# Differential attention on TensorE: both score products of a head ahead of their two masks, and the rotary products of q and k in one instruction each

## The chip, the cores and the metric

The program runs on one core of a Trainium2 chip. The metric is the device time of one execution in microseconds (us), as a median over runs. A profiled execution has a span of its own, from its first instruction to its last, and a time of its own that is a little longer than the span.

## The reference, cut to what matters

A trunk of two layers works on 272 rows (16 learned tokens and 256 inputs) of width 1024. Each layer has a mixer, a layer norm, a feed-forward part (dense in layer 0, eight experts with the two best chosen in layer 1) and a layer norm. The change lies in the attention half of the mixer: four heads, each with two query and key sets of width 64 and one set of values of width 128.

```python
def apply_rope(x, cos, sin):
    x1, x2 = jnp.split(x, 2, axis=-1)
    return x * c + jnp.concatenate([-x2, x1], axis=-1) * s
...
s = jnp.einsum('bqhcd,bkhcd->bhcqk', qb, k).astype(jnp.float32) * scale
causal = kpos[None, :] <= qpos[:, None]
p = jax.nn.softmax(jnp.where(causal, s, -jnp.inf), axis=-1)
a = p[:, :, 0] - lam * p[:, :, 1]
return jnp.einsum('bhqk,bkhe->bqhe', a.astype(v.dtype), v)
```

## The kernel before

**Blocks and slots.** Each mixer first computes its input projection as 24 column blocks in a fixed order (`IN_ORDER`, k and q of heads 0 and 1 first). A block is 24 matmuls on PE: eight slices of the inner dimension, each as three products (`hh`·`whi`, `hl`·`whi`, `hh`·`wlo`, lines 284, 285, 287). The weights arrive by DMA as `raw`; ACT rounds them to `whi` (line 145) and DVE forms the rest `wlo` (line 152), some blocks ahead of PE. The order of all else is written by hand: `Q.at(i, f)` runs step f behind block i, on whichever engines f uses, and the evictions of the blocks follow. Every engine then works through its own instructions in that order.

**The steps of a head b.** `qk[b]` is one tile of 128 partitions by 2 by 272: index 0 holds q, index 1 holds k; partitions 0 to 63 belong to the first of the two sets (c = 0), 64 to 127 to the second (c = 1). `swap` copies `qk[b]` to `rot[b]` by four DMAs with the halves of each 64 exchanged. `rope_cos` multiplies `qk[b]` by the cosines on POOL (line 547), in two instructions, k and then q. `rope` multiplies `rot[b]` by the sines and adds it to `qk[b]` on DVE (lines 553 and 555), in four instructions. In layer 1 the first 16 columns of q aren't needed: a memset has set them to zero, and the instructions on q start at column 16.

**Scores.** `scores(b)` runs behind blocks 10, 12, 14 and 16. It takes up to three tiles t of query rows: 128 rows against 272 keys, 128 rows against 144, and in layer 0 alone 16 rows against 16. For each t and each c it multiplies q by k over 64 partitions in f32 (line 609; each shows as two matmuls in the trace) into the PSUM bank of c, and then adds the causal mask to the diagonal part by a bf16 product of an identity with the mask (line 611). DVE takes the negated row maxima (`mx`, line 621), ACT the exponentials with their sums (line 623). `diff(b)`, one block later, subtracts the second map from the first on DVE (line 634); `a_T(b)`, two blocks behind `scores(b)`, transposes the result on PE (lines 643 to 648); `values(b)` follows a block later.

Of the kernel before, what the change touches and what calls it, by code (L numbers as in the profile page):

```python
# [16 lines left out]
ALU = mybir.AluOpType  # L17
# [3 lines left out]
P = 128  # L21
# [4 lines left out]
T = NMETA + SEQ  # L26
# [161 lines left out]
def body(tc, h0T, consts, vecs, lamv, w_in, w_out, w_gu, w_dn, w_r, mixgb, w_g, w_u, w_d, out, dbg=None):  # L188
    nc = tc.nc
    with ExitStack() as ctx:  # L190
# [9 lines left out]
        def nm(s):  # L200
            uid[0] += 1
            return f"{s}_{uid[0]}"
# [55 lines left out]
        cos = cpre[:, C_COS - C_PRE:C_COS - C_PRE + T]  # L258
        sin = cpre[:, C_SIN - C_PRE:C_SIN - C_PRE + T]
# [12 lines left out]
        def bank(tag="mm", bufs=3):  # L272
            return ps.tile([P, 512], F32, tag=tag, bufs=bufs, name=nm("ps"))
# [220 lines left out]
        def mixer(l, S, Q, before_out=None):  # L494
            c0 = 0 if l == 0 else NMETA
            nq = T - c0
            n2 = max(c0 - 2, 0)
            with tc.tile_pool(name=f"atz{l}", bufs=1) as zp:
# [23 lines left out]
                qk = {}  # L522
# [11 lines left out]
                rot = {}  # L534

                def swap(b):
                    rot[b] = ap.tile([P, 2, T], F32, tag="rot", bufs=2, name=nm("rot"))
                    for p0 in (0, 64):
                        for hf in range(2):
                            d0, s0 = p0 + 32 * hf, p0 + 32 * (1 - hf)  # L540
                            nc.sync.dma_start(rot[b][d0:d0 + 32], qk[b][s0:s0 + 32])

                def rope_cos(b):
                    for j in (1, 0):
                        n0 = c0 if j == 0 else 0
                        x = qk[b][:, j, n0:]
                        nc.gpsimd.tensor_tensor(x, x, cos[:, n0:], ALU.mult)

                def rope(b):
                    for j in (1, 0):  # L550
                        n0 = c0 if j == 0 else 0
                        r = rot[b][:, j, n0:]
                        nc.vector.tensor_tensor(r, r, sin[:, n0:], ALU.mult)
                        x = qk[b][:, j, n0:]
                        nc.vector.tensor_tensor(x, x, r, ALU.add)

                vts = {}

# [44 lines left out]
                def scores(b):  # L603
                    s = [bank("s", 2) for c in range(2)]
                    views = [[s[c][:, :272], s[c][:, 272:416], s[c][:, 416:432]] for c in range(2)]
                    for t, (q0, qn, kn) in enumerate(qt):
                        for c in range(2):
                            pr = slice(c * 64, (c + 1) * 64)
                            nc.tensor.matmul(views[c][t][:qn], qk[b][pr, 0, q0:q0 + qn], qk[b][pr, 1, :kn],
                                             start=True, stop=False)  # L610
                            nc.tensor.matmul(views[c][t][:qn, kn - qn:kn], identb[:qn, :qn], maskb[:qn, :qn],
                                             start=False, stop=True)
                    mx = ap.tile([P, 3, 2], F32, tag="mx", bufs=2, name=nm("mx"))
                    e1 = ap.tile([P, 2, 272], F32, tag="e1", bufs=1, name=nm("e1"))
                    e2 = ap.tile([P, 320], F32, tag="e2", bufs=1, name=nm("e2"))
                    ev = [e1, e2[:, 0:288].rearrange("p (c k) -> p c k", c=2),
                          e2[:, 288:320].rearrange("p (c k) -> p c k", c=2)]
                    es_[b] = ev
                    for t, (q0, qn, kn) in enumerate(qt):
                        for c in range(2):  # L620
                            nc.vector.tensor_reduce(mx[:qn, t, c:c + 1], views[c][t][:qn], AX.X, ALU.max, negate=True)
                        for c in range(2):
                            nc.scalar.activation(ev[t][:qn, c], views[c][t][:qn], AF.Exp, bias=mx[:qn, t, c:c + 1],
                                                 accum_out=sums[:qn, b, t, c:c + 1])
# [75 lines left out]
                for b in range(4):  # L700
                    i = (4, 5, 10, 12)[b]
                    Q.at(i, swap, b)
                    Q.at(i + 1, rope_cos, b)
                    Q.at((8, 9, 12, 14)[b], rope, b)
                    Q.at((8, 9, 14, 15)[b], v_T, b)
                    i = 10 + 2 * b
                    Q.at(i, scores, b)
                    Q.at(i + 1, diff, b)
                    Q.at(i + 2, a_T, b)
                    Q.at(i + 3, values, b)  # L710
                    Q.at(order.index(("h", b)) + 1, conv, b)
# [7 lines left out]
                for i, (t, b) in enumerate(order):  # L719
                    w = W.next()  # L720
                    n0 = c0 if t in "qb" else n2 if t in "ch" else 0
# [99 lines left out]
        Q.at(8, lambda_vals)  # L821
        ln_follow(S0, Q, AF.Exp, 1)
        S1 = mixer(0, S0, Q)
        lpx.close()

# [100 lines left out]
        def prefetch():  # L926
# [3 lines left out]
            W.pump()  # L930

        S3 = mixer(1, S2, Q, prefetch)
        lp = S3.lp
        pre.close()
# [476 lines left out]
```

## Time and profile before

| | us |
|---|---|
| median of 3 runs | 1513.78 |
| lowest and highest run | 1509.94, 1514.09 |
| the profiled execution's own time | 1512.59 |
| its span | 1510.7 |

PE is the TensorE matmul row and PEld its weight loads; matmul durations overlap in the records, so the distance between two starts tells more than the length of one. DVE is VectorE, ACT ScalarE, POOL GpSimd. PE counts as busy for 97% of the span, DVE for 81%, ACT for 66%, POOL for 7%. The input projection and attention of layer 0 lie in the first 130 us, those of layer 1 between some 366 and 467 us, and the experts fill the span from about 500 us on.

### The profile page before, as it was taken

What the parts mean: (1) busy time and instruction counts of PE and PEld (TensorE: products, weight loads), DVE (VectorE), ACT (ScalarE), POOL (GpSimd) and SP (SyncE); (2) the same over time, 40 slices, a digit from 0 to 9 for tenths busy, and PEclk for the clock granted to TensorE, in tenths of its full rate; (3) what the DMA queues carried; (4) which work ended last, traced back from release to release, by engine and by line L of the source; (5) the groups of instructions that cost most, each with busy time, mean ns of one, the idle gap of its engine ahead of it and who ended that gap; (6) DMA issues with size and microseconds to landing.
All of it is one profiled execution on the core that took longest, in us unless ns stands there. A gap on an engine that the chain in (4) does not pass through costs nothing. (4 is left out here: it accounts for less than half of the span.)

```text
span 1510.7 us, 20551 instructions
## 1 busy us (share of the span) xinstructions
PE 1472.8 (97%) x8085; PEld 1272.6 (84%) x8085; DVE 1220.3 (81%) x1210; ACT 998.9 (66%) x1089; POOL 99.1 (7%) x109
## 2 busy tenths in 40 slices
PE   9999999999999899999999999999999999999996
PEld 8789899999889787888888888888888888888885
DVE  7867875465876688898898888889879889888885
ACT  6665464344565577777777777776777777777773
POOL 1202200022102410000000000000000000000001
PEclk9999999999999899999999999999999999999998
DMA  7433264353437588999999999999999999998970
GB/s 258 151 122 138 99 257 151 116 167 155 162 140 277 182 328 334 370 344 376 365 367 364 380 344 348 372 369 359 380 344 347 376 369 370 372 361 333 362 290 30
DMA packets 65240, 427.96 MB, mean 283 GB/s; under 512 B 7520, under 2 KB 11616, under 8 KB 15344
## 3 DMA queue, kind: packets, MB, share of 16 engines
q1 hardware_dynamic: 64672, 426.20, 75.6%
q8 instruction: 65, 1.06, 0.3%
q10 hardware_dynamic: 432, 0.35, 0.1%
q14 instruction: 39, 0.32, 0.1%
q0 software_dynamic: 32, 0.03, 0.0%
HBM read 423.27 MB, written 1.05 MB: 281 GB/s over the span
## 5 line engine op out<-in xcount | busy, mean ns | idle before, releaser
L174 DVE TENSOR_TENSOR wlo<-raw,whi 128x2048 fp32r<-128x2048 f32 x332 | 755.1, 2296 | 119.2 <-ACT whi L173 119.1
L173 ACT ACTIVATE whi<-raw 128x2048 fp32r<-128x2048 f32 x332 | 632.0, 1922 | 152.7 <-PE ps L1069 152.0
L1067 PE MATMUL ps<-whi,xg 128*128 128x512 f32 x896 | 355.6, 397 | 0.0
L1069 PE MATMUL ps<-whi,xg 128*128 128x512 f32 x896 | 350.7, 391 | 2.9 <-POOL xg L1044 2.9
L1068 PE MATMUL ps<-wlo,xg 128*128 128x512 f32 x896 | 350.3, 391 | 0.0
L284 PE MATMUL ps<-hh,whi 128*128 128x272 f32 (+4 forms) x736 | 219.4, 298 | 3.4 <-ACT whi L145 1.5
L285 PE MATMUL ps<-hl,whi 128*128 128x272 f32 (+4 forms) x736 | 216.6, 295 | 4.0 <-DVE hl L394 3.7
L287 PE MATMUL ps<-hh,wlo 128*128 128x272 f32 (+4 forms) x720 | 210.8, 293 | 1.8 <-DVE wlo L152 1.8
L1069 PEld LDWEIGHTS ps<-whi,xg 128*128 128x128 f32 x896 | 168.8, 188 | 39.8 <-POOL xg L1044 3.8
L1067 PEld LDWEIGHTS ps<-whi,xg 128*128 128x128 f32 x896 | 169.2, 189 | 33.1
L152 DVE TENSOR_TENSOR wlo<-raw,whi 128x1024 fp32r<-128x1024 f32 (+2 forms) x148 | 170.3, 1173 | 33.0 <-ACT whi L145 32.9
L1068 PEld LDWEIGHTS ps<-wlo,xg 128*128 128x128 f32 x896 | 169.2, 189 | 32.9
L1069 PE MATMUL ps<-whi,aTl 128*128 128x512 f32 x448 | 174.9, 390 | 2.3 <-DVE aTl L277 2.2
L1067 PE MATMUL ps<-whi,aTh 128*128 128x512 f32 x448 | 175.6, 392 | 0.5 <-ACT aTh L276 0.5
L1068 PE MATMUL ps<-wlo,aTh 128*128 128x512 f32 x448 | 174.7, 390 | 0.0
L145 ACT ACTIVATE whi<-raw 128x1024 fp32r<-128x1024 f32 (+2 forms) x148 | 144.5, 990 | 45.4 <-PE ps L285 37.6
L285 PEld LDWEIGHTS ps<-hl,whi 128*128 128x128 f32 x736 | 142.6, 194 | 6.7 <-DVE hl L394 5.4
L284 PEld LDWEIGHTS ps<-hh,whi 128*128 128x128 f32 x736 | 142.6, 194 | 5.3 <-ACT whi L145 1.7
L287 PEld LDWEIGHTS ps<-hh,wlo 128*128 128x128 f32 x720 | 139.4, 194 | 2.4 <-DVE wlo L152 2.4
L1069 PEld LDWEIGHTS ps<-whi,aTl 128*128 128x128 f32 x448 | 84.1, 188 | 21.1 <-DVE aTl L277 3.6
L1067 PEld LDWEIGHTS ps<-whi,aTh 128*128 128x128 f32 x448 | 84.2, 188 | 17.5 <-ACT aTh L276 0.7
L1068 PEld LDWEIGHTS ps<-wlo,aTh 128*128 128x128 f32 x448 | 84.3, 188 | 16.7
(260 smaller groups left out, 1478.2 us busy)
## 6 DMA issues: line engine op xcount, KB each, us to landing
raw<-in_w_g_dram SPq DMA_DIRECT2D x112, 1024.0 KB, 7.1
raw<-in_w_u_dram SPq DMA_DIRECT2D x112, 1024.0 KB, 7.0
raw<-in_w_d_dram SPq DMA_DIRECT2D x112, 1024.0 KB, 7.2
raw<-in_w_in_dram SPq DMA_DIRECT2D x23, 1024.0 KB, 5.1
raw<-in_w_gu_dram SPq DMA_DIRECT2D x22, 1024.0 KB, 4.8
raw<-in_w_dn_dram SPq DMA_DIRECT2D x16, 704.0 KB, 4.1
raw<-in_w_out_dram SPq DMA_DIRECT2D x8, 1024.0 KB, 4.8
rot<-qk SPq DMA_DIRECT2D x32, 68.0 KB, 4.5
```

The costliest lines, as they stand in the source:

```text
L145: self.nc.scalar.activation(hi, raw, AF.Copy)
L152: self.nc.vector.tensor_tensor(lo, raw, hi.bitcast(F32), ALU.subtract)
L173: self.nc.scalar.activation(hi, raw, AF.Copy)
L174: self.nc.vector.tensor_tensor(lo, raw, hi.bitcast(F32), ALU.subtract)
L284: nc.tensor.matmul(o, w.hi[:, k], xh(k0 + k), start=first and i == 0, stop=False)
L285: nc.tensor.matmul(o, w.hi[:, k], xl(k0 + k), start=False, stop=False)
L287: nc.tensor.matmul(o, w.lo[:, k], xh(k0 + k), start=False, stop=last and i == ka - 1)
L1067: nc.tensor.matmul(o, xh, whi, start=first, stop=False)
L1068: nc.tensor.matmul(o, xh, wlo, start=False, stop=False)
L1069: nc.tensor.matmul(o, xl, whi, start=False, stop=last)
```

## The change

The loop over the two sets c is cut in two, so that for each t both score products are issued first and both masks behind them. The rotary products lose their loop over q and k: one instruction covers both, with the table of cosines or sines repeated by an operand of step 0. In layer 1 these instructions now also cover the first 16 columns of q.

```diff
+                def both(t):
+                    return t.rearrange("p (j t) -> p j t", j=1).to_broadcast([P, 2, T])
+
                 def rope_cos(b):
-                    for j in (1, 0):
-                        n0 = c0 if j == 0 else 0
-                        x = qk[b][:, j, n0:]
-                        nc.gpsimd.tensor_tensor(x, x, cos[:, n0:], ALU.mult)
+                    nc.gpsimd.tensor_tensor(qk[b], qk[b], both(cos), ALU.mult)
 
                 def rope(b):
-                    for j in (1, 0):
-                        n0 = c0 if j == 0 else 0
-                        r = rot[b][:, j, n0:]
-                        nc.vector.tensor_tensor(r, r, sin[:, n0:], ALU.mult)
-                        x = qk[b][:, j, n0:]
-                        nc.vector.tensor_tensor(x, x, r, ALU.add)
+                    nc.vector.tensor_tensor(rot[b], rot[b], both(sin), ALU.mult)
+                    nc.vector.tensor_tensor(qk[b], qk[b], rot[b], ALU.add)
...
                             nc.tensor.matmul(views[c][t][:qn], qk[b][pr, 0, q0:q0 + qn], qk[b][pr, 1, :kn],
                                              start=True, stop=False)
+                        for c in range(2):
                             nc.tensor.matmul(views[c][t][:qn, kn - qn:kn], identb[:qn, :qn], maskb[:qn, :qn],
                                              start=False, stop=True)
```

On PE the place is `scores(0)` of layer 0. Before, the tile of 144 keys stood as follows (`qk_287` is head 0, `ps_691` and `ps_692` are the banks of c = 0 and c = 1; a score product is one row here):

```order
L609 MATMUL ps_691<-qk_287 128x144
L611 LDWEIGHTS identb
L611 MATMUL ps_691<-maskb,identb 128x128
L609 MATMUL ps_692<-qk_287 128x144
L611 LDWEIGHTS identb
L611 MATMUL ps_692<-maskb,identb 128x128
```

Now the same tile reads (the banks have become `ps_685` and `ps_686`, and line 611 has become 608):

```order
L605 MATMUL ps_685<-qk_287 128x144
L605 MATMUL ps_686<-qk_287 128x144
L608 LDWEIGHTS identb
L608 MATMUL ps_685<-maskb,identb 128x128
L608 LDWEIGHTS identb
L608 MATMUL ps_686<-maskb,identb 128x128
```

The product of c = 1 has moved ahead of the mask of c = 0; number and sizes are the same, and so it goes in every tile of every head.

On DVE the place is the rotary part of heads 0 and 1 in layer 0, ahead of the row maxima of head 0. Before (`cpre` holds the sines, `qk_345` and `rot_460` belong to head 1):

```order
L553 TENSOR_TENSOR rot_414<-rot_414,cpre 128x272
L555 TENSOR_TENSOR qk_287<-qk_287,rot_414 128x272
L553 TENSOR_TENSOR rot_414<-rot_414,cpre 128x272
L555 TENSOR_TENSOR qk_287<-qk_287,rot_414 128x272
L152 TENSOR_TENSOR wlo_613<-raw_348,whi_612 128x8x128
L553 TENSOR_TENSOR rot_460<-rot_460,cpre 128x272
L555 TENSOR_TENSOR qk_345<-qk_345,rot_460 128x272
L553 TENSOR_TENSOR rot_460<-rot_460,cpre 128x272
L555 TENSOR_TENSOR qk_345<-qk_345,rot_460 128x272
```

Now:

```order
L550 TENSOR_TENSOR rot_414<-rot_414,cpre 128x544
L551 TENSOR_TENSOR qk_287<-qk_287,rot_414 128x544
L152 TENSOR_TENSOR wlo_609<-raw_348,whi_608 128x8x128
L550 TENSOR_TENSOR rot_459<-rot_459,cpre 128x544
L551 TENSOR_TENSOR qk_345<-qk_345,rot_459 128x544
```

Four instructions of 272 columns have become two of 544 in each head, and nothing has changed its place among the others.

## Rows read from the trace of the kernel before

**Rows 1.** The page, part 1: busy time, share of the span, instructions.

```profile
PE 1472.8 (97%) x8085; PEld 1272.6 (84%) x8085; DVE 1220.3 (81%) x1210; ACT 998.9 (66%) x1089; POOL 99.1 (7%) x109
```

**Rows 2.** PE's waits, 50 to 115 us, then 400 to 460 us.

```profile
PE ps L566 <- ACT aT L654: 0.9, 1, 0.9
...
PE ps L287 <- DVE wlo L152: 0.7, 1, 0.7
```

**Rows 3.** Timeline of PE: scores(0) of layer 0 (start, length, engine, line).

```profile
56.07 0.29 PE L285 MATMUL ps<-hl,whi 128*128 128x272 f32 x1
56.20 0.29 PE L287 MATMUL ps<-hh,wlo 128*128 128x272 f32 x1
56.42 0.72 PE L609 MATMUL ps<-qk 64*128 64x272 f32 x2
57.08 0.23 PE L611 MATMUL ps<-maskb,identb 128*128 128x128 bf16 x1
57.24 0.72 PE L609 MATMUL ps<-qk 64*128 64x272 f32 x2
...
58.05 0.51 PE L609 MATMUL ps<-qk 64*128 64x144 f32 x2
58.49 0.23 PE L611 MATMUL ps<-maskb,identb 128*128 128x128 bf16 x1
58.65 0.51 PE L609 MATMUL ps<-qk 64*128 64x144 f32 x2
...
59.25 0.21 PE L609 MATMUL ps<-qk 64*16 64x16 f32 x2
59.40 0.17 PE L611 MATMUL ps<-maskb,identb 16*16 16x16 bf16 x1
59.49 0.21 PE L609 MATMUL ps<-qk 64*16 64x16 f32 x2
...
59.74 0.39 PE L284 MATMUL ps<-hh,whi 128*128 128x272 f32 x1
```

**Rows 4.** Timeline of PE: the end of scores(0) of layer 1.

```profile
406.31 0.51 PE L609 MATMUL ps<-qk 64*128 64x144 f32 x2
406.75 0.23 PE L611 MATMUL ps<-maskb,identb 128*128 128x128 bf16 x1
406.79 0.37 PE L284 MATMUL ps<-hh,whi 128*128 128x256 f32 x1
```

**Rows 5.** Timeline of DVE: first sine product, next `wlo`, differences of head 0.

```profile
52.52 0.44 DVE L553 TENSOR_TENSOR rot<-rot,cpre 128x272 f32<-128x272 f32 x1
...
54.33 1.22 DVE L152 TENSOR_TENSOR wlo<-raw,whi 128x1024 fp32r<-128x1024 f32 x1
...
65.33 0.91 DVE L634 SCALAR_TENSOR_TENSOR e<-e,cf 128x272 f32<-128x272 f32 x3
```

**Rows 6.** Timeline of PE: first transpose of head 0.

```profile
65.96 0.41 PE L643 MATMUL ps<-cst,e 128*128 128x128 f32 x2
```

**Rows 7.** DVE's waits, 50 to 115 us.

```profile
DVE mx L621 <- PE ps L611: 5.2, 3, 2.2
```

**Rows 8.** Timelines of POOL (cosines of head 2) and DVE (their first use).

```profile
66.33 2.38 POOL L547 TENSOR_TENSOR qk<-qk,cpre 128x272 f32<-128x272 f32 x2 [20.00 <-DMA rot<-qk]
...
73.51 0.44 DVE L555 TENSOR_TENSOR qk<-qk,rot 128x272 f32<-128x272 f32 x1
```

**Rows 9.** Windows: length, busy time of five engines, PE's granted clock, DMA share, GB/s.

```profile
59.70:63.10 3.40, 3.40 (x28) 3.38 (x28) 1.63 (x6) 3.02 (x13) 0.00 (x0) 1.00 0.88 308
...
80.70:84.10 3.40, 3.40 (x21) 1.98 (x19) 1.19 (x4) 0.53 (x2) 0.10 (x1) 1.00 0.47 157
84.10:88.60 4.50, 4.50 (x25) 4.50 (x24) 3.44 (x11) 3.70 (x14) 0.00 (x0) 0.62 0.27 115
...
404.10:407.00 2.90, 2.90 (x15) 1.70 (x15) 1.43 (x2) 0.30 (x2) 0.00 (x0) 1.00 0.75 209
```

## The prediction

> **What bounds the kernel now.** I read the busy times of the whole span first, then PE's waits in the two stretches that the change touches, and then PE's timeline there, start by start. PE is busy for 97% of the span [rows 1]. Where the scores lie it hardly ever waits: one wait of 0.9 us between 50 and 115 us, and a longest one of 0.7 us between 400 and 460 us; the first is for a copy of transposed scores, the second for a weight split ahead of the first score product [rows 2]. So PE's own order is the bound there, and a shorter stretch on PE moves all that follows it, up to the end of the program.
>
> The timeline shows what a score product costs beyond its columns. Blocks of 128 rows follow each other at 0.13 us, but from the last of them (56.20) to the first score product, which uses 64 rows, it takes 0.22 us: 0.09 us more [rows 3]. From there to the mask it takes 0.66 us with 272 columns and 0.44 us with 144 [rows 3]. The difference of 0.22 us is two matmuls of 128 columns, so one pass is 0.23 us for 272 columns and 0.12 us for 144, and a fixed 0.19 us is left in both (0.66 - 0.47, 0.44 - 0.25). I split it into the 0.09 us seen at the change of rows and 0.10 us for a first weight load with nothing ahead of it to hide behind. The tile of 16 columns has 0.15 us, of which some 0.12 is fixed. From a mask to the next score product it takes 0.16 us, or 0.09 with 16 columns [rows 3]. Where a mask is followed by a matmul of the same 128 rows, that matmul's record starts 0.04 us after it [rows 4]. So PE pays at each change between 64 and 128 rows, and before, each of the two sets pays twice.
>
> **The change on PE.** Per tile there were four such changes and two are left: into the pair of score products, and out of it. The second score product of a pair then costs its two passes alone, which saves the fixed 0.19 us. The first mask is followed by the second, of the same rows, so 0.09 of its 0.16 us goes. That is 0.28 us for each of the two large tiles and 0.12 + 0.09 = 0.21 for the small one. A head of layer 0 saves 0.77 us, one of layer 1 (no small tile) 0.56; four of each make 5.3 us.
>
> No row of this trace has two products in a row on different halves of the 64-row arrangement, so this term has bounds. The least: a change of half costs as much as a change of rows, and its load is not hidden. Then only the 0.09 us behind the first mask is saved, 8 x 2 + 4 = 20 times, or 1.8 us. The most: the passes of the second set also run while those of the first do. Then one pass more per pair goes, at most 0.23 + 0.12 us per head, 2.8 us in all, and the term is 8.1. I take 5.3: what costs time in the rows is the change between 64 and 128 rows, and loads between matmuls of one arrangement are hidden in every block [rows 3].
>
> The rows show that a change of rows is paid; they don't show whether a change of half is. The Trainium skill, "TensorEngine Tiling (Array Packing)", section Key Properties, says that changing the tiling mode drains TensorE, and that going to another tile of the same mode does not. By it the term is 5.3 us; by the most cautious reading of the rows alone it is 1.8. No run shows this yet.
>
> **What follows on DVE.** The first row maximum of a head waits for the last mask in the bank of c = 0, which the change brings closer to the end of the group; the group ends earlier by 0.56 to 0.77 us, so that mask is still earlier than before. DVE idles for it in three of the four heads of layer 0, 5.2 us in all [rows 7], so its chain of maxima, exponentials and differences moves forward with PE. Behind these maxima on DVE stand weight splits, and PE doesn't run short of these behind the first score product [rows 2].
>
> Head 0 of layer 0 is the one place where DVE isn't waiting. Its first difference starts at 65.33 and is done some 0.44 us later (three together take 0.91), and PE's first transpose starts at 65.96, 0.19 us behind [rows 5, 6]. PE would come 0.77 us earlier and find nothing. Here the rotary part pays: one head takes 1.81 us on DVE (52.52 to 54.33) [rows 5]. A product of 272 columns is 0.44 us and one of 1024 is 1.22, so a column costs 1.0 ns and 544 columns 0.72 us. With the hop of about 0.1 us between the two and the overlap of 0.08 us at the end, two instructions make 1.46: 0.35 us less per head. Two heads stand ahead of the maxima of head 0, so the chain comes 0.7 us earlier, and PE loses 0.1 us. In the other seven heads the saving on DVE is worth nothing on the path, as PE or ACT sets their pace; without it head 0 would give back 0.7 us.
>
> **POOL.** Two products of 272 columns take 2.38 us with the gap between them; the result is first used at 73.51, 4.8 us after they end at 68.71 [rows 8]. One of 544 columns has the same elements. I put it between half the time (all of it a fixed cost per instruction) and twice the time (the repeated operand read badly), and take the time of now. At twice it would end at 71.1, still 2.4 us early. It costs nothing on the path. The 16 more columns of q in layer 1 are 0.02 us on DVE per instruction.
>
> **The clock.** Behind two of the four groups of scores of layer 0 PE's granted clock is at the lower level, 1.2 GHz, for a while: behind the group of head 2 (80.7 to 84.1, at 1.00) the stretch of 4.5 us has a mean of 0.62 [rows 9]; head 3's, at 98.4 us, reads the same. There 25 matmuls take 4.5 us; at the rate at full clock (28 in 3.4 us) [rows 9] they would take 3.0. Each such stretch costs 1.5 us. Behind the four groups of layer 1, which last 2.7 to 2.9 us and not 3.3 to 3.4, the clock stays at 1.00 (the group of head 0 stands in [rows 9]). After the change a group of layer 0 lasts 3.3 - 0.77 = 2.5 us, shorter than the ones that keep the clock. I take both stretches as gone: 3.0 us. The bounds are 0 and 3.0.
>
> **Sum.** 5.3 - 0.1 + 3.0 = 8.2 us off the profiled execution's 1512.59: 1504.4. The median of the runs lies 1.2 us above the profiled one, which would make it 1505.6. I forecast 1505.0, between the two.
>
> **The rivals.**
>
> (A) The two sets run side by side. Same sum with 2.8 us more: 1502. For it: loads already run under matmuls everywhere. Against it: no row shows two matmuls streaming at once, and the 144-column tile can't gain much, since its 0.12 us pass is little longer than a load of 0.10. The Trainium skill, "TensorE: Matmul & The Clock Gate", section The mechanism, says that matmuls on different row groups run concurrently, a few ns apart. By that rule A holds; the trace bears on it neither way. Chance 0.27.
>
> (B) The order helps as forecast, but the lower clock comes as often, at other places: 1512.6 - 5.2 = 1507.4, or 1508 against the median. For it: the runs before differ by 4 us, which is about three such stretches, so they come and go. Chance 0.15.
>
> (C) A change of half is paid like a change of rows: 1.8 us, with perhaps one of the two slow stretches gone, 1510.5. Chance 0.10.
>
> (D) PE comes earlier and waits: the chain over DVE and ACT keeps its time, and PE meets the differences late in every head as it nearly does in head 0. Then what is left is what DVE itself saves, 8 x 0.35 = 2.8 us: 1511. Against it are the waits of DVE for PE [rows 7]. Chance 0.07.
>
> (E) Slower: POOL reads the repeated operand so badly that the cosines come late. In layer 0 the two products of head 2 have 7.2 us from 66.33 to their use [rows 8]; an instruction that takes longer than that, three times the pair of now, stalls DVE, and behind it the weight splits. It would have to take the 8.2 us back as well, so some 15 us where the pair takes 2.38, to end above 1513. Chance 0.03.
>
> **How the numbers follow.** The forecast has 0.38, its own range 1503 to 1507.5. Bounds of the unknown terms reach from 1502 (A) to 1511 (C and D); with the scatter of the runs, 1500.5 to 1510 leaves out the upper half of C and D, E, and a little at the low end, about 2 in 10. A change within 0.3% (4.5 us, about what a measurement of this kernel can tell) of 1513.78 ends at 1509.2. The forecast, A and most of B lie below that, 0.77; C, D and the rest are the same, 0.19; E and slower stretches of clock 0.04.
>
> **What would show it.** The second score product of a pair should start no more than 0.6 us behind the first at 272 columns (0.82 before), the second mask under 0.1 us behind the first, and a group of layer 0 should last 2.5 us, of layer 1 2.2. If two products of a pair overlap, A is right. The granted clock should stay at 1.00 behind all eight groups. POOL's product should take about 1.9 us and DVE's 0.72. The forecast is wrong if PE shows new waits at the transposes (line 640 after the change), or if the second products start 0.8 us behind the first as before.

## The result, and the profile after

| | before | after |
|---|---|---|
| median of 6 runs each (us) | 1513.76 | 1503.03 |
| lowest to highest run | 1509.94 to 1515.28 | 1500.92 to 1503.74 |
| profiled execution: time, span | 1512.59, 1510.7 | 1502.68, 1500.9 |

The ratio is 0.9932 with a 95% interval of 0.9916 to 0.9947, so the change is faster by 0.68%, more than twice the 0.3% that a measurement can tell.

The page's first part for the changed kernel, which answers to [rows 1]:

```profile
PE 1456.6 (97%) x8085; PEld 1261.3 (84%) x8085; DVE 1220.4 (81%) x1194; ACT 998.6 (67%) x1089; POOL 96.4 (6%) x101
```

The instruction counts show the 16 that DVE lost and the 8 that POOL lost; DVE's busy time hasn't moved. PE has as many matmuls as before.

The timeline of PE in the changed kernel, scores of head 0 in layer 0 (answers to [rows 3]), and then in layer 1 (answers to [rows 4]):

```profile
56.51 0.29 PE L287 MATMUL ps<-hh,wlo 128*128 128x272 f32 x1
56.73 0.73 PE L605 MATMUL ps<-qk 64*128 64x272 f32 x4
57.39 0.28 PE L608 MATMUL ps<-maskb,identb 128*128 128x128 bf16 x2
57.61 0.52 PE L605 MATMUL ps<-qk 64*128 64x144 f32 x4
58.05 0.28 PE L608 MATMUL ps<-maskb,identb 128*128 128x128 bf16 x2
58.27 0.22 PE L605 MATMUL ps<-qk 64*16 64x16 f32 x4
58.42 0.20 PE L608 MATMUL ps<-maskb,identb 16*16 16x16 bf16 x2
58.54 0.40 PE L284 MATMUL ps<-hh,whi 128*128 128x272 f32 x1
...
397.11 0.73 PE L605 MATMUL ps<-qk 64*128 64x272 f32 x4
397.77 0.29 PE L608 MATMUL ps<-maskb,identb 128*128 128x128 bf16 x2
...
398.53 0.37 PE L284 MATMUL ps<-hh,whi 128*128 128x256 f32 x1
```

Read the distance from the first product to the mask: 57.39 - 56.73 = 0.66 us for four matmuls of 272 columns, exactly what two took before; 0.44 us for the four of 144 columns, also as for two before. The whole second product has vanished from PE's time. A narrow window of the timeline of PE, and the same of its weight loads, shows why. In the kernel before it shows one of each:

```profile
56.42 0.49 PE L609 MATMUL ps<-qk 64*128 64x272 f32 x1
```

```profile
56.42 0.18 PEld L609 LDWEIGHTS ps<-qk 64*128 64x128 f32 x1 [0.16 <-issue]
```

In the changed kernel:

```profile
56.73 0.50 PE L605 MATMUL ps<-qk 64*128 64x272 f32 x2
```

```profile
56.73 0.19 PEld L605 LDWEIGHTS ps<-qk 64*128 64x128 f32 x2 [0.15 <-issue]
```

Two matmuls and two loads start at 56.73, where before there was one each; the two matmuls together last 0.50 us, one alone lasted 0.49. A group of scores, from its first product to the next block, falls from 3.32 to 1.81 us in layer 0 and from 2.71 to 1.42 in layer 1, where it began before with

```profile
404.08 0.72 PE L609 MATMUL ps<-qk 64*128 64x272 f32 x2
```

The four groups of a layer last the same. Over the eight groups that is 24.1 to 12.9 us: 11.2 us less on PE.

The end came 9.8 us earlier in the span, although two stretches of lower clock are gone as well. The rest went into new waits. PE's waits between 36 and 480 us, in the kernel before and then in the changed one (what waits, for which engine's work; then the total in us, how often, and the longest):

```profile
PE ps L285 <- DVE hl L394: 3.7, 5, 2.0
PE ps L287 <- DVE wlo L152: 1.8, 2, 1.0
PE ps L285 <- DVE zl L697: 1.5, 2, 0.7
PE ps L566 <- ACT aT L654: 1.4, 2, 0.9
PE ps L284 <- ACT hh L393: 1.2, 1, 1.2
PE ps L284 <- ACT hh L330: 0.7, 1, 0.7
PE ps L693 <- ACT zo L688: 0.7, 1, 0.7
```

```profile
PE ps L285 <- DVE hl L394: 5.3, 5, 2.0
PE ps L562 <- ACT aT L651: 2.1, 2, 1.3
PE ps L287 <- DVE wlo L152: 1.8, 2, 1.0
PE ps L285 <- DVE zl L694: 1.5, 2, 0.7
PE ps L658 <- DVE aT L648: 1.2, 2, 0.7
PE ps L284 <- ACT hh L393: 1.1, 1, 1.1
PE ps L690 <- ACT zo L685: 1.0, 2, 0.7
PE ps L284 <- ACT hh L330: 0.7, 1, 0.7
PE ps L642 <- DVE e L631: 0.7, 1, 0.7
```

They add up to 11.0 and 15.4 us. What has grown is the waits for ACT and DVE behind the scores (transposed scores `aT`, differences `e`) and one ahead of them, for `hl`, to which the experiments come back.

### The profile page after: what moved, and what is told of

Same layout as the page of the kernel before. It is cut to its first block, busy times and chain, and to the rows that moved or that the text cites. A ratio compares the mean times of both kernels' runs of the same rounds, so it can differ in the third digit from the quotient of the medians.

```text
span 1500.9 us, 20523 instructions
## 1 busy us (share of the span) xinstructions
PE 1456.6 (97%) x8085; PEld 1261.3 (84%) x8085; DVE 1220.4 (81%) x1194; ACT 998.6 (67%) x1089; POOL 96.4 (6%) x101
```

## The experiments

The kernels of the first four experiments shared their runs of the kernel before (18 runs, 1509.76 to 1516.58, median 1514.42); the next three shared 11 (1509.49 to 1516.14, median 1511.21); the last had 10 (1509.19 to 1516.27, median 1512.80). So kernels of different groups are compared by the ratio, and two ratios whose intervals overlap are not told apart by it.

**scores_only: the part on PE alone.** The edit against the kernel before:

```diff
                                              start=True, stop=False)
+                        for c in range(2):
                             nc.tensor.matmul(views[c][t][:qn, kn - qn:kn], identb[:qn, :qn], maskb[:qn, :qn],
```

> The change's part on PE alone: both score products of a tile ahead of both masks, the rotary part as in the kernel before. Theory 1 (the two products run side by side on the two halves of the rows, and that is where the time comes from): second product starts under 0.02 us behind the first, a group of scores in layer 0 lasts 1.8 us and not 3.3, and the time falls by nearly all of the whole change's 10.7 us, to 1503 to 1505; head 0 of layer 0 gives up to 0.7 us back, since DVE's chain there stays late. Theory 2 (the rotary part carries the gain by relieving DVE and POOL): no more than 3 us faster, 1510.5 to 1514.

Measured: 1503.96 us (1503.14 to 1504.69), ratio 0.9934, interval 0.9921 to 0.9948. Theory 1 holds: this part alone brings what the whole change brings, within what can be told. PE's waits between 53 and 130 us in this kernel begin with

```profile
PE ps L644 <- DVE e L635: 1.8, 1, 1.8
```

a wait at the first transposes of head 0 in layer 0, which the changed kernel doesn't have in its list. The expectation had put it at 0.7 us; it is 1.8.

**rope_only: the rotary part alone.** The edit is the other half of the change's diff.

> The rotary part alone: one POOL instruction and two on DVE per head, the score products and masks in the order of before. Theory 1: no change, 1512 to 1515, with the PE groups at 3.3 us in layer 0 and 2.7 in layer 1; DVE's two instructions take 0.72 us each. Theory 2: most of the 10.7 us, so 1503 to 1507.

Measured: 1513.79 us (1510.33 to 1518.22), ratio 1.0002, interval 0.9988 to 1.0017: no change, as theory 1 has it.

**same_half: the whole change, but without two halves.** Both products read partitions 0 to 63, so that the scores of the second set are left out.

```diff
-                            pr = slice(c * 64, (c + 1) * 64)
+                            pr = slice(0, 64)
```

> The whole change, but both products of a tile read partitions 0 to 63 (the second set's scores are left out, the first set's stand in both banks); number, sizes and order of all instructions are those of the changed kernel. Theory 1a (different halves of the rows let the products run side by side): here they can't, the second starts about 0.46 us behind the first with 272 columns, a group of layer 0 lasts about 2.5 us (what the forecast had), and the time is 1506 to 1509. Theory 1b (fewer changes between 64 and 128 rows are all that counts, and the close starts in the records only look like an overlap): the same as the changed kernel, 1502 to 1504, with a group of 1.8 us. If the granted clock stays at 1.00 behind groups of 2.5 us, the length of the group is what matters for it; if it falls behind some, it isn't length alone.

Measured: 1508.46 us (1506.55 to 1509.87), ratio 0.9963, interval 0.9950 to 0.9976. The timeline of PE, scores of head 0 in layer 0:

```profile
58.35 1.18 PE L605 MATMUL ps<-qk 64*128 64x272 f32 x4
59.47 0.29 PE L608 MATMUL ps<-maskb,identb 128*128 128x128 bf16 x2
59.68 0.76 PE L605 MATMUL ps<-qk 64*128 64x144 f32 x4
60.37 0.29 PE L608 MATMUL ps<-maskb,identb 128*128 128x128 bf16 x2
60.58 0.26 PE L605 MATMUL ps<-qk 64*16 64x16 f32 x4
60.77 0.20 PE L608 MATMUL ps<-maskb,identb 16*16 16x16 bf16 x2
60.90 0.39 PE L284 MATMUL ps<-hh,whi 128*128 128x272 f32 x1
```

Now it is 1.12 us from the first product to the mask and not 0.66: the second product is back with its two passes, 0.46 us. The group lasts 2.55 us, in layer 1 2.11. This divides the 11.2 us of PE cleanly. With fewer changes between 64 and 128 rows and no second half, the eight groups take 18.6 us, 5.5 less than before; the second half takes off another 5.7. Theory 1a holds and 1b falls.

**The clock in these kernels.** The windows of a group of scores and of the stretch behind it, head 2 of layer 0 in same_half, then head 2 of layer 1 in rope_only (length, busy times, granted clock, DMA share, GB/s):

```profile
81.20:83.80 2.60, 2.60 (x20) 1.69 (x18) 1.02 (x3) 0.53 (x2) 0.10 (x1) 0.99 0.35 76
83.80:88.30 4.50, 4.50 (x26) 4.50 (x24) 3.46 (x9) 3.71 (x14) 0.00 (x0) 0.63 0.45 189
```

```profile
424.50:427.20 2.70, 2.70 (x13) 1.48 (x13) 1.20 (x4) 0.53 (x2) 0.00 (x0) 1.00 0.47 112
427.20:431.00 3.80, 3.80 (x21) 3.80 (x21) 3.17 (x7) 3.21 (x10) 0.00 (x0) 0.55 0.48 201
```

The clock fell to its lower level (1.2 GHz) behind a group of 2.55 us and behind one of 2.71, in executions where the three other groups of that layer kept the clock. In rope_only it also stayed up behind all four groups of layer 0, which last 3.3 us as in the kernel before. In the changed kernel it stayed at 1.00 behind all eight; in scores_only it fell once, within the group of head 1 in layer 0, which follows the wait of 1.8 us above and lasts 2.19 us with the lower clock where its neighbours last 1.8. So neither the length of a group nor the order of its products decides it alone; what does stays open.

**vt_early: a transpose moved out of PE's way.**

```diff
-                    Q.at((8, 9, 14, 15)[b], v_T, b)
+                    Q.at((8, 9, 13, 15)[b], v_T, b)
```

> The changed kernel with the transposes of the values of head 2 one block earlier (slot 13, not 14), where the PSUM buffers that they share with the transposed scores are free. Theory 1 (part of PE's gain is given back at waits of PE that are set by ACT and DVE): the waits of 1.3 and 0.7 us of these transposes for ACT's copies go, and the time falls by 1 to 2 us, to 1501 to 1502. Rival: PE meets the next wait (transposes of head 1 for a free buffer, or values for DVE's copies) with the same loss, 1503.

Measured: 1499.69 us (1499.46 to 1500.85), ratio 0.9908, interval 0.9892 to 0.9924. The waits of line 562 are gone from the list of PE's waits, but another line has grown from 1.2 us:

```profile
PE ps L658 <- DVE aT L648: 2.0, 2, 1.1
```

The list adds up to 14.6 us, only 0.8 less. So the theory holds for the wait, and half of the rival holds too: some of it moved to the next wait. The profiled execution also has one stretch of lower clock fewer in the feed-forward part of layer 0 (the changed kernel has it from 180.4 to 183.8 us), worth 1.5 us, so the gain of 3.2 us over the changed kernel's profiled execution is not all the edit's. All four runs lie below the six of the changed kernel, but the intervals of the two ratios overlap.

**pool_split: the cosines on POOL in two instructions again.** The edit puts back the loop of `rope_cos`; the rest is the changed kernel.

> The changed kernel with the cosine products on POOL split into k and q again (as before); the sines on DVE stay in one instruction. Theory: a DVE instruction that starts during one of POOL's lasts as long as POOL's (0.49 us becomes 1.0 beside POOL's 0.96 and 1.59 beside its 1.54 in the traces so far), so the longer POOL instructions delay PE's first blocks behind slot 7 by about 1 us per layer (waits for hl 3.5 and 0.9 us, 2.4 and 0.4 before), and splitting them gives 0.5 to 1.5 us back: 1501.5 to 1502.5. Rival: DVE loses the same in all (four times 0.5 against two times 1.1), and nothing changes, 1503.

Measured: 1502.59 us (1499.86 to 1503.75), ratio 0.9937, interval 0.9921 to 0.9954. PE's waits for `hl` between 36 and 54 us are

```profile
PE ps L285 <- DVE hl L394: 1.0, 1, 1.0
```

and 3.2 us for the whole stretch from 36 to 480, as against 5.3. The mechanism is there, and 0.9 us of it comes back as a wait for the differences of head 0; on the total the two kernels can't be told apart.

**vt_conv: convolution behind attention.** vt_early, and

```diff
+                for b in range(4):
                     Q.at(order.index(("h", b)) + 1, conv, b)
```

> The kernel vt_early (values of head 2 transposed one block earlier), and the convolution steps of a slot registered behind the attention steps, so that DVE copies the transposed scores of head 3 ahead of two convolution products of 1.0 us. Theory: PE's waits for DVE's copies (1.0 and 1.1 us in vt_early) shrink by their whole length, 1497.5 to 1498.5. Rival: the chain to the end of the mixer (convolution, head scale, last split) is what counts, and PE waits there as much longer: 1499.7.

Measured: 1499.41 us (1497.96 to 1500.33), ratio 0.9918, interval 0.9903 to 0.9934. PE's waits for DVE's copies are gone, and the wait for the scaled heads (`zo`) has gone from 1.0 to

```profile
PE ps L690 <- ACT zo L685: 2.0, 2, 1.2
```

No faster than vt_early, as the rival had it, but only in part for its reason: of the 2.0 us of waits that are gone 1.0 came back there, and PE's waits add up to 12.9 us, 1.7 less than in vt_early. The profiled execution has a stretch of lower clock, from 117.8 to 121.2 us, that vt_early's doesn't have. Why the median didn't move stays open.

**cos_dve: the cosines on DVE.** vt_conv, and

```diff
-                    nc.gpsimd.tensor_tensor(qk[b], qk[b], both(cos), ALU.mult)
+                    pass
...
+                    nc.vector.tensor_tensor(qk[b], qk[b], both(cos), ALU.mult)
                     nc.vector.tensor_tensor(rot[b], rot[b], both(sin), ALU.mult)
```

> vt_conv with the cosine products moved from POOL to DVE, just ahead of the sines. Theory of the turns that DVE and POOL take: each POOL instruction of 1.54 us held a DVE instruction 1.1 us longer, while on DVE the product costs 0.72 us, so DVE gains 0.4 us per head, the waits for hl fall to 0.5 to 1 us per layer, and the time is 0.5 to 2 us under vt_conv. Rival: 1.5 us more on DVE just ahead of the row maxima of head 0 delays PE's first transposes by as much, and the time is 1 us or more above vt_conv.

Measured: 1497.59 us (1494.60 to 1499.73), ratio 0.9909, interval 0.9893 to 0.9924. The timeline of DVE shows the eight instructions that form `hl` in one row, undisturbed; between 53 and 130 us PE's longest wait is now the one that the rival named:

```profile
42.42 3.39 DVE L394 SCALAR_TENSOR_TENSOR hl<-h,vec,hh 128x272 fp32r<-128x272 f32 x8
```

```profile
PE ps L641 <- DVE e L632: 2.2, 1, 2.2
```

Both happened. DVE's eight instructions took 3.4 us here and 5.6 us in the changed kernel,

```profile
41.64 5.58 DVE L394 SCALAR_TENSOR_TENSOR hl<-h,vec,hh 128x272 fp32r<-128x272 f32 x8
```

and part of that is given back at head 0. All six runs lie below all six of the changed kernel. Against vt_conv, from which it differs by this edit alone, the runs overlap and the ratios can't be told apart. The profiled execution is 3.4 us shorter than vt_conv's, but up to 130 us it also has 6.8 us less at the lower clock (3.4 between 43 and 50 us and 3.4 from 117.8 us on), worth some 3 us by the 1.5 us of the stretches before; whether the edit brought that isn't shown.

**cos_dve_late: the rotary part of head 1 later.** cos_dve, and

```diff
-                    Q.at((8, 9, 12, 14)[b], rope, b)
+                    Q.at((8, 11, 12, 14)[b], rope, b)
```

> cos_dve with the rotary part of head 1 two slots later on DVE (slot 11, behind the differences of head 0 and not ahead of its row maxima). Theory (PE's time gained in the scores is worth what the chain of maxima, exponentials and differences lets through): the wait of 2.2 us of PE's transposes of head 0 in layer 0 goes, and the time falls 1 to 2 us under cos_dve, to 1495.5 to 1496.5. Rival: the rotary part of head 1 now stands late for its own scores behind block 12, PE waits there for 1 us or more in each layer, and nothing is gained, 1497.6 or above.

Measured: 1498.80 us (1498.07 to 1500.97), ratio 0.9909, interval 0.9891 to 0.9928: nothing gained. The first line of PE's waits is now

```profile
PE ps L606 <- DVE qk L552: 3.0, 2, 1.6
```

PE stands ahead of the score products of head 1, once in each layer, as the rival had it. Still, PE's waits add up to 11.2 us, less than the 12.1 of cos_dve. What the profiled execution lost on cos_dve's (4.8 us) it lost mainly with the clock, in four stretches of 3.4 us at the lower level between 60 and 410 us, where cos_dve's has none. Two of them begin right behind the group of head 1, in layer 0 and in layer 1 (windows as above, the clock third from the end):

```profile
66.90:70.60 3.70, 3.70 (x20) 3.70 (x19) 2.74 (x8) 3.12 (x13) 0.00 (x0) 0.54 0.17 41
405.10:408.50 3.40, 3.40 (x18) 3.40 (x17) 2.75 (x7) 2.76 (x10) 0.00 (x0) 0.51 0.27 62
```

As in scores_only, the group before them followed a wait of PE, here of 1.6 and 1.4 us. But a wait isn't enough either: in cos_dve PE waited 2.2 us at the transposes ahead of the same group of layer 0 and kept the clock.

## Why the prediction was right, and where it was off

It forecast 1505.0, in 1500.5 to 1510.0, and faster; the median is 1503.03. Step by step:

- **PE bounds these stretches, and a shorter one moves what follows.** Right in the main: 11.2 us came off PE's groups and 9.9 off the time of the profiled execution, with the clock's 3.0 us on the one side and 4.4 us of new waits on the other.
- **Fewer changes between 64 and 128 rows: 5.3 us.** Right, shown by same_half: 5.5 us, a group of 2.55 us where 2.5 was forecast, and a second product that costs its two passes (0.46 us) and nothing else. How the 0.19 us per product divides between the change of rows and the load isn't shown. The rule of the Trainium skill, "TensorEngine Tiling (Array Packing)", section Key Properties, that going to another tile of the same mode costs no drain, agrees with the changed kernel's pairs: 0.66 us for two products as for one.
- **The second half.** The term was mis-sized: the forecast took 0 and bounded it at 2.8 us, by one pass per pair; it measured 5.7. The bound went wrong by letting only one of the second product's two passes run beside the first product. Loads and passes of both run side by side from the start, at 56.73 us, and in the tile of 144 columns as well, where rival A expected little. Rival A, with its chance of 0.27, names the mechanism, at half of its worth; the rule that it quotes from the Trainium skill, "TensorE: Matmul & The Clock Gate", section The mechanism, agrees with the trace, where two products on different halves start at the same 56.73 us.
- **DVE's chain moves with PE.** Partly. Head 0 lost little, as forecast: the rotary part took 1.47 us on DVE (1.46 forecast). Without it, in scores_only, PE waited 1.8 us there. But the other heads were taken to follow without loss. PE came 1.5 us per head earlier and not 0.77, and met waits at transposes, differences and copies. PE's waits grew by 4.4 us in all; that is rival D in part.
- **POOL costs nothing on the path.** Off. The cosines were not late: a product took 1.35 to 1.90 us, where about 1.9 was forecast. (The 2.38 us of the two products before held no gap: one took 1.67 us beside a weight split on DVE, the other 0.75.) But the forecast looked only at who needs their result, and not at what runs beside them; see the last section. PE's waits for `hl` grew by 1.6 us, and shrank by 2.1 with the split instructions of pool_split.
- **The clock, 3.0 us.** It came out so in the profiled pair: no lower clock behind any of the eight groups. But the reason given, that shorter groups keep it, doesn't stand: it fell behind groups of 2.55 and 2.71 us in other kernels, and behind shorter ones in cos_dve_late. Of the median's gain less may be the clock's. Eight runs of the kernel before, made beside the experiments, had a mean granted clock of 0.990 and took 1509.91 to 1511.58 us (median 1510.5); the three of the changed kernel with 0.990 took 1500.92 to 1502.68 (median 1502.2). That is 8.3 us at the same clock and leaves some 2 of the 10.7 us for the clock, an estimate from few runs.

The sum of the profiled execution: -11.2 on PE's groups, -3.0 for the two stretches of lower clock and +4.4 of waits make -9.8, and 9.9 was measured (the stretch of the experts differs by less than 1 us between the two). The forecast's sum of 8.2 came close with 5.9 us too little on PE and 4.3 too little for the waits: two errors that nearly cancel, and that is luck.

## What to carry to other kernels

Products over 64 rows come in pairs: put those of the two halves next to each other and keep everything of other shape out from between them; the second cost nothing here, where the two went into different banks (no run tried one bank). When PE gets faster in one place, look for what each of its next steps waits for: here about two fifths of what PE gained went into waits on ACT and DVE, and moving one step by a block took 2.1 us of these waits away, of which most came back at other steps. An instruction on an idle engine isn't free because nobody waits for it: ask whose instructions run beside it.

## What the runs showed of the hardware

DVE and POOL hold each other up. In the changed kernel POOL runs its first two products of 544 columns from 41.8 us on, and in these 3.05 us DVE gets no more than two of its instructions done (the timeline of POOL, and that of DVE between 42 and 43 us, with the two instructions that it shows there):

```profile
41.80 3.05 POOL L547 TENSOR_TENSOR qk<-qk,cpre 128x544 f32<-128x544 f32 x2 [14.28 <-ACT hh L393]
```

```profile
41.64 2.00 DVE L394 SCALAR_TENSOR_TENSOR hl<-h,vec,hh 128x272 fp32r<-128x272 f32 x2
```

The group of these DVE instructions between 41 and 46 us shows shortest, middle and longest:

```profile
L394 DVE SCALAR_TENSOR_TENSOR hl<-h,vec,hh x6: 490/494/1590, 41.6 to 45.9; 128x272 fp32r<-128x272 f32 x6
```

The one that started ahead of POOL took 0.49 us; one that came during an instruction of POOL took 1.59, and POOL's own took 1.54. "SBUF — State Buffer" of the Trainium skill, section Who interferes with whom, says that a DVE instruction with two SBUF inputs contends with one of GpSimd that reads SBUF; the trace agrees. The same happens later to the differences of head 0 in layer 1:

```profile
403.64 1.87 DVE L631 SCALAR_TENSOR_TENSOR e<-e,cf 128x272 f32<-128x272 f32 x2
```

with one of POOL's from 403.88 to 405.35. These took 1.22 us before, beside a shorter POOL instruction. POOL is held as well, where DVE came first: one product began during a weight split on DVE and took longest of the eight, the others 1.35 to 1.57 us:

```profile
65.69 1.90 POOL L547 TENSOR_TENSOR qk<-qk,cpre 128x544 f32<-128x544 f32 x1 [20.85 <-DMA rot<-qk]
```

So a product of 544 columns on POOL held one DVE instruction back by about 1.0 to 1.1 us (in seven cases of eight), more than the 0.72 us that the product takes on DVE itself. In cos_dve DVE has eight instructions more than in vt_conv, and its busy time is 1.9 us less (1216.2 and 1218.1 us).
